# First stage of a hybrid block: later transposes for the second token block of a third, and a recurrence at 1.6 steps a block, begun at unit ten

## The chip, the cores and the metric

The kernel runs on one core of one Trainium2 chip. A core has a matmul engine (TensorE, PE in the rows of a profile, with its weight loads as PEld), a vector engine (DVE), a scalar engine (ACT), GpSimd (POOL) and SyncE (SP), whose queue issues nearly all DMAs here. Each engine works through its own list of instructions in a fixed order and stops where the next one has to wait. The metric is the device time of one execution, in microseconds (us); less is better.

## The reference, cut to what matters

One layer over T = 2064 tokens (16 learned meta tokens and 2048 of the input) of width 1024, all in float32:

```python
h = concat([meta, x])                         # (2064, 1024)
p = rms_norm(h, norm_mix_pre) @ w_in          # columns of three head groups
oa = rg_lru_group(...)        # gated linear recurrence over time, 256 columns
ob = forgetting_attention_group(q, k, v, f)   # 8 heads of 64, causal
oc = rwkv7_group(...)         # state S <- S*w - (S kk)(kk a) + v k, one step a token, 256 columns
mixed = concat([oa, ob, oc]) @ w_out
h = h + rms_norm(mixed, norm_mix_post)
f = causal_dwconv(rms_norm(h, norm_ffn_pre) @ ffn_up, ffn_conv)
h = h + rms_norm((gelu(gate) * val) @ ffn_down, norm_ffn_post)
```

The change is in how the first product, `rms_norm(h) @ w_in`, and the two recurrences that read it (`oc`, here called the recurrence, with `oa` beside it) are laid out in time. What is computed stays the same.

## The kernel before, in words

A float32 product is made of three matmuls in a shorter format: every operand is kept as a high and a low half (`xh`, `xl`, `wh`, `wl`), and L174, L175 and L176 multiply high by high, low by high and high by low. The first stage (the projection) computes `p` transposed, with 128 columns of `w_in` as the stationary operand and up to 400 tokens moving.

The tokens are cut into three thirds ("parts" in the code, 0 to 2), and each third into two token blocks: 400 and 384 tokens, 384 and 384, 256 and 256. For a third, `w_in_norm` loads token tiles of 128 rows (L127), takes the sum of squares on ACT (L119) and a short chain on DVE (L86 to L95), scales the tile (L132), and `transpose_split` turns it on PE (L145, eight transposes of 128x128 for a tile, four to a PSUM bank, tile `pst`), after which ACT writes the high half (L151) and DVE the low half (L152). The operands `xh0`, `xl0` (first block) and `xh1`, `xl1` (second block) have one buffer each, and the raw token tiles share four buffers (pool `nt`).

Then `w_in_part` runs 25 units over the third: first the eight forget-gate columns (`w_in_gate`, matmuls L293 and L294 into `psf`), then 24 units of 128 columns (8 of kind "c" for the recurrence, 4 "a" for the gated linear one, 4 each of k, v and q). A unit is one step (24 matmuls into `psp`) for each token block, and results go to DRAM. The weights of a unit are split once, in the first third, and read back ready-made in the others. From the first to the last third the two steps of a unit have 400 + 384, 384 + 384 and 256 + 256 tokens.

The recurrence reads these results back. It works on nine blocks of 256 tokens (the ninth has 64), three to a third. Written as a generator (`recurrences`), it is cut into steps: two for the forget gates of the third, then for each block four steps of preparation (its matmuls are L1040, L1051, L1115, L1144; then fifteen rounds between POOL and DVE, L1162 and L1163), ten steps that end the block before (L1186, L1228, L1238, L1253, L1265, L1273, L1304, L1309, L1333), and four of the linear recurrence (L1424, L1425). `Beside` is the pace-maker: after each projection step `advance()` adds `PACE` to a count and runs that many whole steps of the generator. The generator of a third is put in when 14 units of it are done, in the first third as in the others. What is left over after the last third is run by `beside.finish()`, ahead of the attention in the program.

The program's text is not the final order. A scheduler places every instruction, engine by engine: what stands earlier in the text has precedence, and what is not ready by its reckoning lets later work past. So recurrence matmuls stand between projection matmuls, and after the projection between those of the attention. The attention (L561 maxima, L688 and L689 scores, L711 values) takes heads in two halves of query blocks; when its first half is done, matmuls of the output projection (`pswo`) fill PE beside its second half.

Of the kernel before, what the change touches and what calls it, by code (L numbers as in the profile page):

```python
# [119 lines left out]
    return rstd_from(core.nc, v, ss, width, core.apart)  # L120


def norm_transpose(core, pools, psum, src, rows, gain, pieces, after=nullcontext):

    nc = core.nc
    xt = pools["nt"].tile([P, D], F32, tag="nt_x", name=core.n("xt"))
    nc.sync.dma_start(xt[:rows], src)  # L127
# [4 lines left out]
    nc.vector.scalar_tensor_tensor(xt[:rows], xt[:rows], rs, gain[:rows], op0=ALU.mult, op1=ALU.mult)  # L132
    transpose_split(core, psum, xt, rows, pieces)


def transpose_split(core, psum, xt, rows, pieces):

    nc = core.nc
    for k0 in range(0, KD, 4):
        ps = psum.tile([P, 4, P], F32, tag="mm", name=core.n("pst"))
        for k in range(4):
            nc.tensor.transpose(  # L145
                ps[:, k, :rows], xt[:rows, (k0 + k) * P : (k0 + k + 1) * P], core.ident[:rows, :rows]
            )
        ks = slice(k0, k0 + 4)
        for hi, lo, c, r0, n in pieces:
            ds_, ss_ = slice(c, c + n), slice(r0, r0 + n)  # L150
            nc.scalar.activation(hi[:, ks, ds_], ps[:, :, ss_], AF.Copy)  # L151
            nc.vector.tensor_tensor(lo[:, ks, ds_], ps[:, :, ss_], hi[:, ks, ds_], op=ALU.subtract)  # L152
# [36 lines left out]
def w_in_norm(core, pools, psum, x, meta, gain, part):  # L189
    blocks = []  # L190
    for b, tl in enumerate(w_in_tokens(part)):
        t0 = tl[0][0]
        n = sum(r for _, r in tl)
        hi = pools["xn"].tile([P, KD, n], F32R, tag=f"xh{b}", name=core.n("xh"))
        lo = pools["xn"].tile([P, KD, n], F32R, tag=f"xl{b}", name=core.n("xl"))
        blocks.append((t0, n, tl, hi, lo))
    for t0, n, tl, hi, lo in blocks:
        for s, rows in tl:
            src = meta if s < META else x[s - META : s - META + rows, :]
            late = part == 1 and (s, rows) not in blocks[0][2][:2]  # L200
            after = (lambda: core.tc.issue_after(core.rounded.ins)) if late else nullcontext
            norm_transpose(core, pools, psum, src, rows, gain, [(hi, lo, s - t0, 0, rows)], after)
    return blocks


def w_in_kept(scr, c0):
# [65 lines left out]
    return turn  # L272


def w_in_gate(core, pools, psum, w_in, blocks, scr, part):

    nc = core.nc
    c0 = 2048
    w = pools["w"].tile([P, KD, P], F32R, tag="wh", name=core.n("fw"))
    flat, kept = w[:].rearrange("p k c -> p (k c)").bitcast(F32), w_in_kept(scr, 3 * D)[0]  # L280
    if part == 0:
        raw = pools["st"].tile([P, KD, 8], F32, tag="stv", name=core.n("fraw"))
        nc.sync.dma_start(raw[:], w_in[:, c0 : c0 + 8].rearrange("(k p) c -> p k c", p=P))
        nc.vector.memset(w[:].bitcast(F32), 0.0)
        nc.scalar.activation(w[:, :, 0:8], raw[:], AF.Copy)
        nc.vector.tensor_tensor(w[:, :, 32:40], raw[:], w[:, :, 0:8], op=ALU.subtract)
        nc.sync.dma_start(kept, flat)
    else:
        nc.sync.dma_start(flat, kept)
    for t0, n, tl, hi, lo in blocks:  # L290
# [9 lines left out]
    yield False  # L300
    yield True


def w_in_part(core, pools, psum, w_in, blocks, scr, part):
    yield from w_in_gate(core, pools, psum, w_in, blocks, scr, part)
    units = [("c", 2056 + P * i) for i in range(8)] + [("a", P * i) for i in range(4)]
    units += [(s, c + P * i) for s, c in (("k", 1024), ("v", 1536), ("q", 512)) for i in range(4)]
    waiting = [None]

    def step(*args):  # L310

        after = w_in_step(core, pools, psum, *args, scr)
        if waiting[0]:
            waiting[0]()
        waiting[0] = after

    for kind, c0 in units[:-2]:
        w = w_in_weights(core, pools, w_in, c0, scr, part)
        for block in blocks:
            step(w, block, kind, c0)  # L320
            yield block is blocks[-1]

    last = [(w_in_weights(core, pools, w_in, c0, scr, part), kind, c0) for kind, c0 in units[-2:]]
    for block in blocks:
        for w, kind, c0 in last:
            step(w, block, kind, c0)
            yield kind == "q" and c0 == last[-1][2]
# [1681 lines left out]


READY = 13
PACE = 1.25

WIDE = (0, 5)

# [5 lines left out]
class Beside:  # L2021
# [54 lines left out]
def hybrid_block_kernel(ctx: ExitStack, tc: tile.TileContext, args, out):  # L2076
# [25 lines left out]
    with ExitStack() as p1:  # L2102
# [7 lines left out]
        with ExitStack() as p1a:  # L2110
# [4 lines left out]
            split_out = w_out_split(core, pools["nt"], a["w_out"], scr)  # L2115
            following = w_in_norm(core, pools, ps_mm, x, meta, g_pre, 0)
            for part in range(3):
                blocks = following
# [5 lines left out]
                units = w_in_part(core, pools, ps_mm, a["w_in"], blocks, scr, part)  # L2124
                for _ in range(READY if part == 0 else 0):
                    while not next(units):
                        pass
# [19 lines left out]
                    beside = Beside(PACE)  # L2147
                i = READY + 1 if part == 0 else 1
                for whole in units:
                    if whole and i == READY + 1:  # L2150
                        beside.add(recurrences(core, R, lk, a["fox_f_bias"], scr, blocks, part))
                    beside.advance()
                    if not whole:
                        continue
                    if part == 1 and i > 1:
                        next(split_out, None)
                    if part and i % 2 == 0:
                        with tc.issue_after(core.loaded.ins):
                            next(sums, None)
                    i += 1  # L2160
# [184 lines left out]
```

## Time and profile before

| what | us |
|---|---|
| median of 3 runs | 3020.2 (3015.82 to 3026.11) |
| the profiled execution | 3012.84 |
| its span, first to last instruction | 3011.1 |
| last projection matmul of the first, second, last third ends | 278.5, 613.1, 874 |
| first projection matmul of the second third starts | 321.1 |
| last recurrence matmul ends | 1125 |
| first output projection matmul starts | 1193 |

The times of the last four rows are read from the timeline of PE in the trace. A row of the table by stretches gives the stretch, its length, then for each engine its busy time and the number of its records, the mean granted PE clock (1.00 is full speed), the DMA share and the rate. With a tile's or a line's name it counts the instructions on that tile or line alone. The records of recurrence matmuls are those on the tiles `rps` and `eps`; many of them are float32 and leave two records for one matmul.

### The profile page before, as it was taken

To read this page: it belongs to the slowest core of one execution; us is meant where nothing else is said; L and a number is where in the kernel's file an instruction comes from. 1 tells how busy PE (TensorE), PEld (TensorE's weight loads), DVE (VectorE), ACT (ScalarE), POOL (GpSimd) and SP (SyncE) were. 2 spreads that over 40 slices of the span, in tenths; PEclk is the share of its full clock that TensorE was granted. 3 is DMA by queue.
4 is the path that set the end of the run, shared out by engine and by line. 5 is a ranking of instruction groups with operands and counts; after the bars stand their busy time and mean duration, and the time that the engine had idled before them with its cause. 6 is when DMAs were issued, how large, how long until landed. Compare 5 with 4: busy or idle time off the path is not lost.

```text
span 3011.1 us, 52783 instructions
## 1 busy us (share of the span) xinstructions
PE 2901.2 (96%) x18694; PEld 2487.0 (83%) x18694; DVE 2039.1 (68%) x3937; ACT 1479.4 (49%) x2858; POOL 1314.8 (44%) x1567
## 2 busy tenths in 40 slices
PE   6999999999999999999989999999999999999998
PEld 6998899888886654566558999999999999787887
DVE  5258645665577775555626898798778777656766
ACT  4246333444346654454635666666666665424333
POOL 1002121222124666566843567455644534656443
PEclk8999999999978999999999999999999999999999
DMA  6776569576653347435326565577777764436453
GB/s 212 236 240 217 164 227 310 183 236 218 188 135 81 97 109 212 111 96 124 82 76 230 167 203 177 171 209 211 215 210 218 214 199 131 162 116 220 139 180 119
DMA packets 469190, 530.49 MB, mean 176 GB/s; under 512 B 85710, under 2 KB 355736, under 8 KB 467372
## 3 DMA queue, kind: packets, MB, share of 16 engines
q1 hardware_dynamic: 468156, 526.17, 57.9%
q8 instruction: 147, 2.41, 0.3%
q14 instruction: 119, 0.97, 0.1%
q0 software_dynamic: 768, 0.93, 0.1%
HBM read 368.07 MB, written 158.90 MB: 175 GB/s over the span
## 4 chain that ended last, share of the span: by engine, by line
PE 44%; DVE 2%; DMA 1%; POOL 1%; ACT 1%; issue 1%; SPq 0%; DVEq 0%; POOLq 0%; ACTq 0%
PE psu L174 9%; PE psu L175 9%; PE psu L176 9%; PE psd L174 4%; PE psd L175 4%; PE psd L176 4%; PE pswo L174 1%; PE pswo L176 1%; PE pswo L175 1%; PE pst L1604 1%; DMA uq<-scr_us 0%; POOL dw L1638 0%; DVE uw L1638 0%; PE po L711 0%; POOL u L1903 0%
## 5 line engine op out<-in xcount | busy, mean ns | idle before, releaser
L174 PE MATMUL psu<-xo,uw 128*128 128x344 f32 x1848 | 586.6, 322 | 6.4 <-ACT ga L1809 3.3
L175 PE MATMUL psu<-xo,uw 128*128 128x344 f32 x1848 | 592.2, 321 | 0.0
L176 PE MATMUL psu<-xo,uw 128*128 128x344 f32 x1848 | 581.8, 320 | 0.0
L174 PE MATMUL psp<-xh,wh 128*128 128x384 f32 (+2 forms) x1152 | 380.4, 330 | 0.0
L176 PE MATMUL psp<-xh,wl 128*128 128x384 f32 (+2 forms) x1152 | 377.9, 328 | 0.2 <-DMA wl<-scr_wk 0.2
L175 PE MATMUL psp<-xl,wh 128*128 128x384 f32 (+2 forms) x1152 | 377.2, 327 | 0.0
L1638 DVE TENSOR_TENSOR uw<-uq,uw 128x512 fp32r<-128x512 f32 x341 | 324.9, 957 | 58.0 <-ACT uw L1637 55.2
L174 PEld LDWEIGHTS psu<-xo,uw 128*128 128x128 f32 x1848 | 346.4, 188 | 8.1 <-ACT ga L1809 3.6
L175 PEld LDWEIGHTS psu<-xo,uw 128*128 128x128 f32 x1848 | 347.7, 188 | 0.0
L176 PEld LDWEIGHTS psu<-xo,uw 128*128 128x128 f32 x1848 | 346.2, 188 | 0.0
L1637 ACT ACTIVATE uw<-uq 128x512 fp32r<-128x512 f32 x462 | 288.1, 627 | 94.0 <-PE psu L176 42.9
L693 ACT ACTIVATE p<-sc,bias 128x512 f32<-128x512 f32 (+4 forms) x352 | 197.4, 589 | 187.4 <-PE sc L689 161.4
L566 DVE TENSOR_REDUCE mc<-mx 128x1 f32<-128x512 f32 (+6 forms) x352 | 190.2, 565 | 112.8 <-PE mx L561 85.8
L1777 DVE SCALAR_TENSOR_TENSOR uy<-psu,ffn_cols,uy 128x342 f32<-128x342 f32 (+1 forms) x390 | 220.4, 567 | 59.9 <-ACT uy L1775 57.9
L1785 POOL TENSOR_TENSOR uy<-uy,uy 128x342 f32<-128x342 f32 (+1 forms) x132 | 145.4, 1102 | 240.6 <-DVE uy L1777 59.7
L732 POOL TENSOR_TENSOR acc<-acc,p 128x512 f32<-128x512 f32 (+3 forms) x208 | 221.3, 1067 | 52.1 <-DVE acc L732 24.7
L1638 POOL TENSOR_TENSOR uw<-uq,uw 128x512 fp32r<-128x512 f32 x121 | 177.9, 1470 | 138.8 <-ACT uw L1637 121.1
L174 PEld LDWEIGHTS psp<-xh,wh 128*128 128x128 f32 x1152 | 220.0, 191 | 8.3 <-issue 6.9
L176 PEld LDWEIGHTS psp<-xh,wl 128*128 128x128 f32 x1152 | 219.8, 191 | 7.6 <-issue 5.1
L175 PEld LDWEIGHTS psp<-xl,wh 128*128 128x128 f32 x1152 | 219.9, 191 | 5.0 <-issue 3.2
L1638 DVE TENSOR_TENSOR fo<-u,fo 128x896 fp32r<-128x896 f32 x88 | 101.7, 1155 | 132.0 <-ACT fo L1637 131.5
L1637 ACT ACTIVATE fo<-u 128x896 fp32r<-128x896 f32 x88 | 81.2, 923 | 205.9 <-PE psd L176 117.3
(483 smaller groups left out, 6415.2 us busy)
## 6 DMA issues: line engine op xcount, KB each, us to landing
uq<-scr_us SPq DMA_DIRECT2D x220, 256.0 KB
uq<-in_ffn_up_dram SPq DMA_DIRECT2D x209, 256.0 KB
wl<-scr_wk SPq DMA_DIRECT2D x48, 512.0 KB
wh<-scr_wk SPq DMA_DIRECT2D x48, 512.0 KB
u<-scr_ff SPq DMA_DIRECT2D x88, 256.0 KB
scr_ff<-uy SPq DMA_DIRECT2D x110, 171.0 KB
raw<-in_w_in_dram SPq DMA_DIRECT2D x24, 512.0 KB
scr_wk<-wh SPq DMA_DIRECT2D x24, 512.0 KB
```

What stands on the lines that cost most here:

```text
L174: nc.tensor.matmul(out, ah, bh, start=first, stop=False, skip_group_check=more)
L175: nc.tensor.matmul(out, ah, bl, start=False, stop=False, skip_group_check=more)
L176: nc.tensor.matmul(out, al, bh, start=False, stop=last, skip_group_check=more)
L566: self.reduced = nc.vector.tensor_reduce(mc[:rows, i, ci : ci + 1], ps[:rows, : e - a], axis=AX.X, op=ALU.max)
L693: last = nc.scalar.activation(p[:rows, :w], ps[:rows, :w], AF.Exp, bias=bias[:rows, j : j + 1])
L732: eng.tensor_tensor(a, ps_[0][0][:rows, c0:n] if start and i == 1 else a, p[:rows, : n - c0], op=ALU.add)
L1604: nc.tensor.transpose(ps[:, k, :rows], xt[:rows, k0 : k0 + P], core.ident[:rows, :rows])
L1637: core.nc.scalar.activation(hi, src, AF.Copy)
L1638: (eng or core.nc.vector).tensor_tensor(lo, src, hi, op=ALU.subtract)
L1777: core.conved = stt(y[:, :n], src[:, i : n + i], cw[:, 44 * i + cc : 44 * i + cc + 1], y[:, :n], op0=ALU.mult, op1=ALU.add)
L1785: core.pooled = nc.gpsimd.tensor_tensor(v[:, :n], g[:, :n], v[:, :n], op=ALU.mult)
```

## The change

There are four parts.

- `norm_transpose` is split into `normed` (load, norm, scale) and the transposes. In the second and third third the token tiles of the second token block are normed where they were, but their transposes are put off until the first block has gone through the gate and the first unit.
- The gate is no longer a pass over both blocks ahead of the units. Its matmuls for a block stand ahead of that block's step of the first unit. The yields of the first unit are such that the count of units stays the same.
- `PACE` goes from 1.25 to 1.6 steps of the recurrence for each projection step.
- In the second and third third the generator is put in after ten units in place of fourteen. In the first third it stays at fourteen.

```diff
-def norm_transpose(core, pools, psum, src, rows, gain, pieces, after=nullcontext):
+def normed(core, pools, src, rows, gain, after=nullcontext):
...
-    transpose_split(core, psum, xt, rows, pieces)
+    return xt
...
-    for t0, n, tl, hi, lo in blocks:
+    waiting = []
+    for b, (t0, n, tl, hi, lo) in enumerate(blocks):
...
-            norm_transpose(core, pools, psum, src, rows, gain, [(hi, lo, s - t0, 0, rows)], after)
-    return blocks
+            xt = normed(core, pools, src, rows, gain, after)
+            waiting.append((core, psum, xt, rows, [(hi, lo, s - t0, 0, rows)]))
+            if part == 0 or b == 0:
+                transpose_split(*waiting.pop())
+    return blocks, waiting
...
     for kind, c0 in units[:-2]:
         w = w_in_weights(core, pools, w_in, c0, scr, part)
         for block in blocks:
+            if gate:
+                gate(block)
+                yield block is blocks[-1]
             step(w, block, kind, c0)
+            while normed:
+                transpose_split(*normed.pop(0))
             yield block is blocks[-1]
+        gate = None
...
-PACE = 1.25
+PACE = 1.6
...
-                    if whole and i == READY + 1:
+                    if whole and i == (10 if part else READY + 1):
                         beside.add(recurrences(core, R, lk, a["fox_f_bias"], scr, blocks, part))
```

Where PE goes over from the first to the second third, the end of its list before reads as follows (`pst` are transposes of token tiles, `rps` and `eps` recurrence matmuls, `psf` the gate, `psp` the projection; numbers are buffers).

```order
L1040 MATMUL eps_3340<-rwwa_3315,wa_up 128x256 x2
L145 MATMUL pst_3226<-ident,xt_3211 128x128 x4
L145 MATMUL pst_3233<-ident,xt_3211 128x128 x4
L1051 MATMUL eps_3348<-rwsq_3345,gat 4x256 x2
L1186 MATMUL rps_2573<-rwxf_2341,rwxu_2297 32x32 x16
L1228 MATMUL rps_2591<-rww_202_1645,rwsc_1644 64x64 x8
L145 MATMUL pst_3255<-ident,xt_3240 128x128 x4
L145 MATMUL pst_3262<-ident,xt_3240 128x128 x4
L293 MATMUL psf_3271<-xh_3091,fw_3269 128x384
L294 MATMUL psf_3271<-xl_3092,fw_3269 128x384
```

The first gate matmul stands behind the transposes of all six tiles; no `psp` matmul of the second third stands ahead of these rows. After the change (line numbers are 6 higher for the gate and 12 higher from L330 on) the gate of the first block comes behind the third tile:

```order
L1156 MATMUL rps_2128<-ident,rwbk_2030 128x128 x4
L1156 MATMUL rps_2134<-ident,rwrav_2023 128x128 x4
L145 MATMUL pst_3476<-ident,xt_3454 128x128 x4
L299 MATMUL psf_3534<-xh_3392,fw_3528 128x384
L1198 MATMUL rps_2227<-rwxu_2218,rwsc_1644 32x32 x32
L1052 MATMUL eps_2970<-rwwa_2951,wa_up 128x256 x2
L300 MATMUL psf_3534<-xl_3393,fw_3528 128x384
```

and the other three tiles come behind the 24 matmuls of the first unit's first step:

```order
L174 MATMUL psp_3594<-xh_3392,wh_3530 128x384
L175 MATMUL psp_3594<-xl_3393,wh_3530 128x384
L176 MATMUL psp_3594<-xh_3392,wl_3531 128x384
L145 MATMUL pst_3622<-ident,xt_3483 128x128 x4
L145 MATMUL pst_3629<-ident,xt_3483 128x128 x4
L145 MATMUL pst_3636<-ident,xt_3498 128x128 x4
L145 MATMUL pst_3643<-ident,xt_3498 128x128 x4
L1198 MATMUL rps_2411<-rwxf_2225,rwxu_2218 32x32 x16
L1240 MATMUL rps_2466<-rww_202_1645,rwsc_1644 64x64 x8
L145 MATMUL pst_3650<-ident,xt_3513 128x128 x4
```

So 24 of the 48 transposes moved behind 16 gate and 24 projection matmuls. The second to third crossing moves in the same way, with 16 of 32 transposes.

The other place is the end of the projection on PE. Before, behind the last `psp` matmul stands the end of the sixth recurrence block, with its late lines L1253 to L1304:

```order
L175 MATMUL psp_10080<-xl_6567,wh_9817 128x256
L176 MATMUL psp_10080<-xh_6566,wl_9818 128x256
L1238 MATMUL rps_9191<-rww_973_7341,rwxf_8880 64x128 x4
L1253 MATMUL rps_9237<-rwsc_7340,rwxu_9169 64x128 x8
L1091 MATMUL eps_9753<-rwsq_9660,bones 128x512
L1253 MATMUL rps_9248<-rwsc_7340,rwxu_9169 64x128 x8
L1265 MATMUL rps_9260<-rww_973_7341,rwsc_7340 64x64 x16
L1273 MATMUL rps_9260<-rstate,rwgt_9235 64x64 x4
L1304 MATMUL rps_9298<-rstate,rwrav_7292 64x64
```

After the change it is the seventh block that begins its ending there (L1198 was L1186), and the preparation of the ninth (L1052, 64 tokens) stands beside it:

```order
L175 MATMUL psp_10681<-xl_7194,wh_10439 128x256
L176 MATMUL psp_10681<-xh_7193,wl_10440 128x256
L1156 MATMUL rps_9391<-ident,rwbk_9311 128x128 x4
L1156 MATMUL rps_9397<-ident,rwrav_9304 128x128 x4
L1156 MATMUL rps_9403<-ident,rwbk_9311 128x128 x4
L1156 MATMUL rps_9409<-ident,rwrav_9304 128x128 x4
L1198 MATMUL rps_9491<-rwxu_9482,rwsc_8363 32x32 x32
L1052 MATMUL eps_10196<-rwwa_10177,wa_up 128x64 x2
L1198 MATMUL rps_9558<-rwxu_9482 32x32 x16
L1198 MATMUL rps_9576<-rwxu_9482 32x32 x32
```

Counted over the whole built list of PE, 2304 recurrence matmuls are there in both kernels. Before, 668 of them stand behind the last projection matmul, after the change 557. The fourth block, the first of the second third, begins behind 1867 of the 3456 projection matmuls before, behind 1637 after. The last recurrence matmul stands behind 108 of the attention's 352 score matmuls of L688 before, behind 63 after; the first output projection matmul stands behind 146 and behind 152 of them.

More of the change, by code (lines that the diff above doesn't have):

```diff
@@ L272, in w_in_step, with w_in_gate @@
     return turn
-def w_in_gate(core, pools, psum, w_in, blocks, scr, part):
+def w_in_gate(core, pools, psum, w_in, scr, part):
     nc = core.nc
@@ L289, in w_in_gate, with step @@
         nc.sync.dma_start(flat, kept)
-    for t0, n, tl, hi, lo in blocks:
+    def step(block):
+        t0, n, tl, hi, lo = block
         ps = psum.tile([P, 512], F32, tag="mm", name=core.n("psf"))
@@ L299, in w_in_gate, with w_in_part @@
         nc.sync.dma_start(scr["f"][:, t0 : t0 + n], o[:, :n])
[L300 to L305, printed above, removed]
+    return step
+def w_in_part(core, pools, psum, w_in, blocks, scr, part, normed):
+    gate = w_in_gate(core, pools, psum, w_in, scr, part)
     units = [("c", 2056 + P * i) for i in range(8)] + [("a", P * i) for i in range(4)]
@@ L2117, in hybrid_block_kernel @@
             for part in range(3):
-                blocks = following
+                blocks, late = following
                 if part == 0:
@@ L2123, in hybrid_block_kernel @@
                         nc.gpsimd.dma_start(scr["p"][r : r + P, 0:PAD], zeros[:])
-                units = w_in_part(core, pools, ps_mm, a["w_in"], blocks, scr, part)
+                units = w_in_part(core, pools, ps_mm, a["w_in"], blocks, scr, part, late)
                 for _ in range(READY if part == 0 else 0):
```

## The prediction

> **What bounds the kernel now.** I read the page first, then stretches of the first stage, then who waits for whom.
>
> ```profile
> span 3011.1 us, 52783 instructions
> PE 2901.2 (96%) x18694; PEld 2487.0 (83%) x18694; DVE 2039.1 (68%) x3937; ACT 1479.4 (49%) x2858; POOL 1314.8 (44%) x1567
> PE   6999999999999999999989999999999999999998
> PEclk8999999999978999999999999999999999999999
> ```
>
> PE is busy for 96% of the span, so its work is the bound nearly everywhere. A change that only moves work can win back two things: time in which PE is idle, and time in which it runs at less than its full clock. The clock row shows the second in the 12th and 13th of its 40 slices of 75 us, where the projection hands over to the attention. Finer stretches show more (length; PE, PEld, DVE, ACT, POOL busy; clock; DMA):
>
> ```profile
> 278.50:321.10 42.60, 37.01 (x388) 30.56 (x387) 37.22 (x101) 26.67 (x51) 13.59 (x20) 0.72 0.39 119
> 288.60:312.50 23.90, 21.73 (x257) 17.19 (x250) 20.96 (x63) 16.25 (x31) 9.40 (x13) 0.50 0.26 91
> 613.10:619.70 6.60, 4.42 (x35) 3.58 (x34) 5.33 (x12) 4.99 (x12) 2.96 (x4) 1.00 0.90 268
> 619.70:623.10 3.40, 3.40 (x18) 3.40 (x17) 2.21 (x6) 0.47 (x2) 0.00 (x0) 0.50 1.03 395
> 628.30:874.00 245.70, 239.83 (x2572) 218.58 (x2571) 158.07 (x405) 107.58 (x220) 57.68 (x91) 0.98 0.61 188
> 874.00:1047.00 173.00, 162.24 (x1489) 113.89 (x1488) 132.10 (x368) 93.45 (x208) 85.90 (x137) 0.81 0.44 104
> 1047.00:1125.00 78.00, 72.40 (x528) 45.11 (x527) 59.93 (x155) 46.56 (x96) 47.03 (x74) 0.98 0.43 101
> 1125.00:1193.00 68.00, 60.36 (x272) 30.32 (x271) 39.98 (x88) 29.71 (x54) 36.45 (x43) 0.90 0.78 218
> ```
>
> The first row is the crossing from the first to the second third, from the last projection matmul of the one to the first of the other. In its 42.6 us PE is idle for 5.6 us, and at a clock of 0.72 it loses about 0.28 x 42.6 = 12 us more (one of them counted already, since 2.2 us of the half-clock stretch in the second row are idle). The crossing loses 16.5 us. The other crossing loses 2.2 us idle (third row) and half of 3.4 us at half clock (fourth): 3.9 us. The last third (fifth row) loses little. Behind the projection, 874 to 1193, what is left of the recurrence runs among the attention's first half, and the clock is 0.81 to begin with.
>
> How the attention and the recurrence share that time is seen by counting: score matmuls of L688 (PE, PEld only), then recurrence matmuls on `rps`, then on `eps`, in two stretches each:
>
> ```profile
> 874.00:1047.00 173.00, 24.40 (x62) 12.18 (x63) 0.81 0.44 104
> 1047.00:1125.00 78.00, 18.65 (x52) 9.05 (x51) 0.98 0.43 101
> 1125.00:1193.00 68.00, 13.91 (x34) 6.32 (x33) 0.90 0.78 218
> 1450.00:1500.00 50.00, 15.90 (x41) 7.48 (x41) 1.00 0.33 73
> ...
> 874.00:1047.00 173.00, 67.44 (x1046) 56.82 (x1044) 25.71 (x57) 12.19 (x25) 0.81 0.44 104
> 1047.00:1125.00 78.00, 13.90 (x220) 10.33 (x220) 7.34 (x24) 2.91 (x7) 0.98 0.43 101
> ...
> 874.00:1047.00 173.00, 8.88 (x36) 5.55 (x36) 3.13 (x9) 4.08 (x12) 0.81 0.44 104
> ```
>
> Until 1125 us PE executes 1046 + 220 + 36 = 1302 recurrence records and 114 score matmuls. Then 34 scores take 68 us without any recurrence, and late in the attention 41 scores take 50 us, with nothing beside them.
>
> **The change part by part.** First the price of a recurrence record inside the projection, from the last third (tiles `rps`, then `eps`):
>
> ```profile
> 628.30:874.00 245.70, 74.54 (x1346) 62.43 (x1347) 33.92 (x68) 19.26 (x38) 0.98 0.61 188
> 628.30:874.00 245.70, 23.63 (x85) 12.46 (x85) 9.62 (x23) 10.89 (x26) 0.98 0.61 188
> ```
>
> That is 98.2 us for 1431 records, 69 ns each. Behind the projection it is (67.44 + 8.88 + 13.90) / 1302, again 69 ns. The built lists put 668 recurrence matmuls behind the last projection matmul before, 557 after; 668 are 1302 records, so the 111 moved are 216 records.
>
> *Pace and earlier start, cost.* The projection ends later by 216 x 69 ns = 14.9 us: PE is full there, so nothing hides them. The last third's idle time, 245.7 - 239.8 = 5.9 us on 1431 records, adds 4 ns to each, 1 us. Sum +16. DVE and ACT carry their share beside it (158 and 108 us busy of 246). A step brings its DMAs to SP with it, but PE's waits for weights in these thirds come to one row (below).
>
> *Pace and earlier start, gain.* After the change the attention reaches its 63rd score with 557 x 1.95 = 1086 records done; before, it reached the 62nd at 1047 us with 1082 done. The same work in the same mixture: 173 us, no gain. From there to the 114th it took 78 us beside 220 records; now none are left. Two rows bound what that saves. If PE sets the pace, the records' own 13.9 us go. If the attention then runs as at 1450 us, 52 scores take 52 x 50 / 41 = 63.4 us, and 14.6 us go. If the chain of maxima, exponentials and sums sets the pace, nothing goes. I take -14, because PE was busy for 72.4 of the 78 us, and keep 0 and -15. From the 114th score on nothing changes: the first output projection matmul stands behind 146 scores before and 152 after.
>
> *Late transposes, first crossing.* Nothing is removed: 48 transposes, 32 gate matmuls and the recurrence stay. But the first gate matmul no longer stands behind the sixth tile, whose transposes ran at 308.8:
>
> ```profile
> 280.90 1.07 ACT L151 ACTIVATE xh<-pst 128x512 fp32r<-128x512 f32 x2
> 281.98 1.28 DVE L152 TENSOR_TENSOR xl<-pst,xh 128x512 fp32r<-128x512 f32 x2
> 284.22 1.15 SPq L127 DMA_DIRECT2D xt<-in_x_dram  x2
> ...
> 300.31 1.97 PE L145 MATMUL pst<-ident,xt 128*128 128x128 f32 x8 [0.47 <-DVE xt L132]
> 308.77 1.97 PE L145 MATMUL pst<-ident,xt 128*128 128x128 f32 x8
> 321.13 0.34 PE L174 MATMUL psp<-xh,wh 128*128 128x384 f32 x1
> ```
>
> The last two tiles were late because their loads wait for raw buffers that the first two tiles free, and went out at 284.2 (third row here). Meanwhile 40 dense matmuls (16 gate, 24 projection) now fill PE, so the half clock should end some 10 us sooner than at 312.5. I take 5 us of lost clock and 3 us of idle time as what remains of the 16.5 (the first three tiles' copies, 1.3 us a tile on DVE by the row at 281.98, still stand between their transposes and the gate): -8.5. Bounds: -3, if copying keeps PE waiting, and -14.
>
> *Second crossing.*
>
> ```profile
> 612.98 3.62 PE L145 MATMUL pst<-ident,xt 128*128 128x128 f32 x28
> 618.76 0.66 PE L145 MATMUL pst<-ident,xt 128*128 128x128 f32 x4 [2.16 <-DVE xl L152]
> ```
>
> There 28 transposes ran at once and PE then waited 2.16 us for a bank. Now 16 go, with four banks, and recurrence matmuls stand in the hole. Of 3.9 us I take -3; bounds 0 and -4.
>
> *Gate inside the first unit, first third.* The same matmuls in another order; no transpose moves. 0, hidden by nothing and needing nothing; at worst a weight that is late, 0.2 us by the row below.
>
> Sum: +16 - 14 - 8.5 - 3 = -9.5. The profiled execution took 3012.8 (span 3011.1 and 1.7 around it), 7.4 under the median, so the like execution would take 3003.3, and the median goes to 3020.2 - 9.5, about 3010. The extremes of the terms give +16 - 0 - 3 - 0 = +13 and +16 - 15 - 14 - 4 = -17.
>
> A rule speaks against this. The Trainium skill, "TensorE: Matmul & The Clock Gate", section "Part 4: PE-mode transpose", says that transposes do not count as busy time for the clock. The fourth row above agrees: after 32 transposes the clock is halved for 3.4 us, although it stayed full while they ran.
>
> **The rivals.**
>
> *Transposes in the middle cost a clock window.* The late transposes stand between dense matmuls, 24 of them with 36 small recurrence matmuls about them at the first crossing. If such a stretch halves the clock once, as at 619.7, each crossing pays half of 3.4 us: 2 x 1.7 = 3.4, hence -6, 3014. The rule quoted is this mechanism. For it: the fourth row. Against it: the transposes of the first crossing are now split in two.
>
> *The attention's chain is the limit.* Then the last 52 scores gain nothing: +16 - 11.5 = +4.5, 3025. For it: 1125 to 1193, 34 scores in 68 us, half a score a us, slower than with the recurrence. Against it: 41 in 50 us later, and that slow stretch is where the attention changes halves and DMA is at 0.78.
>
> *The recurrence stalls the projection, and it gets slower.* In the lists after the change the blocks follow each other by 340 to 370 projection matmuls in the second third (377 to 442 before), as close as their own dependencies let them in the scheduler's reckoning. A recurrence matmul that is not ready holds up the projection behind it. The waits of PE from 150 to 874 us were small:
>
> ```profile
> PE rps L1186 <- DVE rwxu L1203: 6.5, 5, 2.1
> PE rps L1186 <- ACT rwsc L1145: 1.9, 2, 1.7
> PE psp L176 <- DMA wl<-scr_wk: 0.2, 1, 0.2
> ```
>
> But where the recurrence runs unpaced, 874 to 1047, PE is idle for 10.8 of 173 us, 6.2%, against 2.4% in the last third. If the projection from 281 to 874 us goes the same way, it loses 3.8% of 593 = 22 us: +13, 3033. It decides once PE's idle share there is up by 1.6% (9.5 us). The Trainium skill, in the same page under "Part 2: What happens when you issue a matmul", says that matmuls stay in program order; the waits above are that order at work.
>
> *The handover warms up.* The 0.81 of 874 to 1047 is 33 us of lost clock. If dense projection matmuls up to the end and a shorter tail save a third of it, the gain is 20: 3000 or less.
>
> **How the numbers follow.** Chances: the forecast 0.50 (its own range 2998 to 3022: -17 and, with both crossings at their lesser bounds, -1, and some 4 us of scatter at each end), transposes that cost a window 0.08, the attention's chain 0.14, stalls 0.22, a warmer handover 0.06. About 0.3%, 9 us, is what a measurement of this kernel can tell from no change; the runs shown spread by 10. Of the forecast 0.38 lies under 3011, since its largest unknowns (how long the clock stays halved at the first crossing, what a moved record costs) reach further down. With the warm handover that makes faster 0.44. Within 9 us: the rest of the forecast 0.12, transposes 0.08, most of the attention's chain 0.10, 0.30. Slower: stalls 0.22 and 0.04 of the chain, 0.26. The range runs from 2995, which takes in the forecast and a part of the warm handover, to the stalls' 3033, and leaves out half of the stalls.
>
> **What would show it.** Right: at the first crossing a half clock that ends before 303 us in place of 312.5; the projection ending near 878 (874 + 16 - 11.5); recurrence matmuls ending near 1050; the first output projection matmul near 1183. Wrong: a PE idle share over 4% from 330 us to the projection's end, or waits of `psp` or `rps` there of 15 us or more in all; the first output projection matmul behind 1193 in spite of a projection that ends on time.

## The result and the profile after

The kernel got slower. Over 16 runs of each, the median is 3028.9 us after the change (3023.96 to 3046.66) and 3018.1 us before (3012.41 to 3026.11): ratio 1.0044, 95% interval 1.0034 to 1.0055. The profiled execution took 3028.55 us. The page of the kernel after, to set beside the one shown of before:

```profile
span 3026.7 us, 52801 instructions
PE 2904.5 (96%) x18694; PEld 2497.7 (83%) x18694; DVE 2034.5 (67%) x3937; ACT 1483.2 (49%) x2858; POOL 1315.2 (43%) x1567
PE   6999999999998988999989999999999999999998
PEclk8999999999996989999999999999999999999999
```

Every engine has the work that it had. The dip of the clock where the projection hands over to the attention stands in the 13th of 40 slices, with a smaller one in the 15th, in place of the 12th and 13th, since the projection ends later. The page doesn't show where 16 us went; stretches cut at the same places of the program do. They are, first before and then after: 50 us from the end of the first third's projection, the inside of the second third, 20 us around the second crossing, the inside of the last third, and from the projection's end to the first output projection matmul (columns as in the prediction: length; busy us of PE, PEld, DVE, ACT, POOL; clock; DMA).

```profile
278.50:328.50 50.00, 44.41 (x445) 36.89 (x445) 42.55 (x113) 28.29 (x55) 14.11 (x21) 0.76 0.37 112
328.50:608.10 279.60, 277.35 (x2316) 253.99 (x2313) 151.82 (x368) 97.58 (x183) 56.13 (x83) 0.99 0.72 237
608.10:628.10 20.00, 17.82 (x145) 16.56 (x144) 13.73 (x36) 7.60 (x17) 2.96 (x4) 0.91 0.92 311
628.10:873.70 245.60, 239.73 (x2572) 218.48 (x2572) 158.07 (x405) 107.49 (x220) 57.68 (x91) 0.98 0.61 189
873.70:1193.00 319.30, 295.30 (x2287) 189.61 (x2287) 232.01 (x610) 169.96 (x356) 169.38 (x252) 0.87 0.51 128
```

```profile
277.10:327.10 50.00, 46.85 (x535) 39.72 (x534) 43.85 (x114) 28.06 (x56) 14.57 (x22) 0.97 0.50 161
327.10:634.60 307.50, 296.14 (x2478) 268.63 (x2478) 181.20 (x453) 122.99 (x232) 64.71 (x98) 0.96 0.68 220
634.60:654.60 20.00, 19.87 (x206) 17.22 (x199) 16.11 (x33) 7.09 (x14) 4.03 (x5) 0.83 0.55 183
654.60:910.80 256.20, 246.58 (x2485) 223.89 (x2485) 149.19 (x385) 94.79 (x197) 49.28 (x77) 0.96 0.59 180
910.80:1217.30 306.50, 275.89 (x2091) 179.62 (x2090) 209.17 (x551) 163.78 (x338) 169.91 (x253) 0.88 0.51 133
```

Length less PE's busy time is idle time, and length times what the clock lacks to 1.00 is lost clock; their sum is called the loss below (the clock taken unrounded from the trace). Two things about it: idle time inside a stretch of half clock is counted in both terms (up to 1.7 us in a row shown here), and half clock comes in stretches of 3.4 us or multiples of it in the projection here, so the lost clock goes in steps of 1.7 us. In the first row the loss falls from 17.5 to 4.9 us: the first crossing gained. In the second row it rises from 4.0 to 25.0: 11.4 us idle where 2.3 were, and 13.7 us of lost clock where 1.7 were. In the fourth it rises from 11.7 to 19.9. The projection ended at 910.8 us in place of 873.7. The last row got 13 us shorter, and what follows it 9 us (4 and 11 in a second profile of each kernel).

What PE waited for in the two thirds after the change, and how the longest wait comes about: first the five largest of PE's waits from 327 to 911 us (us in total, times, longest), then ACT's and PE's instructions around one of them, then the stretch behind it.

```profile
PE eps L1052 <- ACT rwe L1054: 5.6, 2, 3.0
PE rps L1198 <- DVE rwix L1175: 4.9, 2, 2.9
PE rps L1198 <- DVE rwxu L1215: 2.8, 1, 2.8
PE psp L174 <- DMA wh<-scr_wk: 2.6, 1, 2.6
PE eps L1436 <- ACT rwlg L1440: 1.7, 1, 1.7
```

```profile
513.11 0.47 ACT L244 ACTIVATE sth<-psp 128x384 fp32r<-128x384 f32 x1
513.59 1.28 ACT L1452 ACT_TABLE_LOAD   x1
514.89 0.42 ACT L1452 ACTIVATE rwlr<-rwlr 128x256 f32<-128x256 f32 x1
515.32 1.28 ACT L1054 ACT_TABLE_LOAD   x1
516.62 0.84 ACT L1054 ACTIVATE rwe<-eps,rwkv_om 128x256 f32<-128x256 f32 x2
...
514.16 0.34 PE L175 MATMUL psp<-xl,wh 128*128 128x384 f32 x1
517.51 1.22 PE L1052 MATMUL eps<-rwwa,wa_up 64*128 64x256 f32 x2 [3.01 <-ACT rwe L1054]
```

```profile
515.60:522.50 6.90, 4.99 (x13) 4.16 (x14) 5.95 (x12) 4.32 (x9) 4.70 (x7) 0.51 0.37 109
```

The second pair of matmuls of L1052 needs the one `eps` buffer, which L1054 on ACT has to empty first. On ACT stands, in between, an instruction of the gated linear recurrence (L1452) that uses another function table. So the table is exchanged twice, 1.28 us each time, PE stands still for 3.0 us with projection matmuls queued behind, and its clock is halved for 6.9 us, from 1.1 us into the wait on. The kernel before loads tables about as often in these thirds (31 times, 32 after) and has no wait of PE for ACT above 0.2 us from 328 to 874 us; so it isn't their number, but where they stand. (The Trainium skill, "ScalarE: Activation LUTs", section "What ACT_TABLE_LOAD costs", gives 1283 ns for the load and about 1380 ns more for a drain. The load agrees, but here ACT was busy until 513.58 and again from 514.89, so that no such drain shows.)

The waits for DVE are of the same kind. PE's row and DVE's list ahead of it, for one of them:

```profile
832.78 1.22 DVE L1071 TENSOR_TENSOR rwe<-rwe 128x512 f32<-128x512 f32 x1
834.30 0.25 DVE L1175 TENSOR_REDUCE rwix<-rwitmp 128x8 f32<-128x88 f32 x1 [0.30 <-POOL rwitmp L1174]
834.47 0.52 DVE L1097 COPY rwwc<-rwe 128x8 f32<-128x8 f32 x1
834.90 0.41 DVE L1462 SCALAR_TENSOR_TENSOR rwlr<-rwlr,rwlraw 128x256 f32<-128x256 f32 x1
835.35 0.54 DVE L1463 SCALAR_TENSOR_TENSOR rwlu<-rwlu,rwlr 128x256 f32<-128x256 f32 x1
835.82 0.67 DVE L1215 TENSOR_TENSOR rwxu<-rps,rwxu 32x512 f32<-32x512 f32 x1
...
836.55 0.68 PE L1198 MATMUL rps<-rwxu,rwsc 32*32 32x32 f32 x9 [2.83 <-DVE rwxu L1215]
```

L1215 is a step in the end of one block. Ahead of it stands work of other blocks: preparation (L1071, L1097), a round (L1175, which waited for POOL in its turn) and the linear recurrence (L1462, L1463).

### The profile page after: what moved, and what is told of

Its sections match the earlier page's. It is cut to its first block, busy times and chain, and to the rows that moved or that the text cites. A ratio compares the mean times of both kernels' runs of the same rounds, so it can differ in the third digit from the quotient of the medians.

```text
span 3026.7 us, 52801 instructions
## 1 busy us (share of the span) xinstructions
PE 2904.5 (96%) x18694; PEld 2497.7 (83%) x18694; DVE 2034.5 (67%) x3937; ACT 1483.2 (49%) x2858; POOL 1315.2 (43%) x1567
## 5 line engine op out<-in xcount | busy, mean ns | idle before, releaser
L1174 POOL TENSOR_TENSOR rwitmp<-rwix,rwia 128x16 f32<-128x16 f32 (+9 forms) x135 | 67.6, 501 | 268.9 <-DVE rwia L1169 189.7
```

What stands on the lines that cost most here:

```text
L1174: nc.gpsimd.tensor_tensor(m3, x3[:, :, : t + 1], a3[:, t : t + 1, : t + 1].to_broadcast([np_, jw, t + 1]), op=ALU.mult)
```

## The experiments

All experiments share one set of measures: the ratio to the kernel before, and the loss by the four stretches named above. At the outset there were three theories. T1: the recurrence at its new pace and start stalls the projection, and the gain at the crossings is real. T2: the new order of the transposes costs by itself. T3: nothing stalls; work was moved and the gains were given back elsewhere.

The results together (us of loss; two values are two profiles of the same kernel; "order" names the thirds that have the late transposes):

| kernel | pace, start, order | first crossing | inside second third | second crossing | inside last third | ratio to before |
|---|---|---|---|---|---|---|
| before | 1.25, 14, none | 17.5, 18.5 | 4.0, 5.7 | 3.9, 1.5 | 11.7, 10.3 | 1 |
| after | 1.6, 10, both | 4.9, 7.0 | 25.0, 26.7 | 3.5, 0.0 | 19.9, 17.8 | 1.0044 [1.0034, 1.0055] |
| e_order | 1.25, 14, both | 8.7 | 4.0 | 4.0 | 20.2 | 0.9987 [0.9968, 1.0005] |
| e_rec | 1.6, 10, none | 19.0 | 12.0 | 6.5 | 15.0 | 1.0047 [1.0030, 1.0063] |
| e_pace | 1.6, 14, both | 5.3 | 15.0 | 3.2 | 18.5 | 1.0010 [0.9989, 1.0030] |
| e_start | 1.25, 10, both | 9.3 | 3.9 | 7.9 | 22.1 | 1.0013 [0.9995, 1.0030] |
| e_alone | none in the last two thirds, both | 7.0 | 1.1 | 0.4 | 12.9 | 1.0492 [1.0478, 1.0506] |
| e_lru | 1.6, 10, both | 7.0 | 13.4 | 8.4 | 10.5 | 1.0230 [1.0215, 1.0246] |
| e_half | 1.25, 14, second | 12.3 | 2.9 | 2.0 | 14.8 | 0.9974 [0.9956, 0.9991] |
| e_slow | 1.0, 14, both | 9.4 | 4.4 | 4.8 | 8.2 | 1.0067 [1.0054, 1.0081] |
| e_mid | 1.4, 14, second | 8.7 | 12.6 | 2.1 | 14.4 | 1.0004 [0.9989, 1.0019] |
| e_last | 1.6, 10, second | 4.5 | 30.2 | 0.0 | 13.1 | 1.0038 [1.0026, 1.0051] |

**The parts apart.** Four kernels, each with a part of the change. The order alone:

```diff
-PACE = 1.6
+PACE = 1.25
...
-                    if whole and i == (10 if part else READY + 1):
+                    if whole and i == READY + 1:
```

> The order of the second token block alone (pace 1.25, generator put in after 14 units, as in the kernel before). Theory 1, the recurrence stalls the projection: the crossings keep what the changed kernel's trace shows there (a loss of 5.9 us between 250 and 350 us in place of 17.3), the rest of the projection is as before, so 8 to 12 us less than before, a ratio of 0.996 to 0.997. Theory 2, the order itself costs (raw buffers and projection banks held longer, the second crossing split into small pieces): the projection ends 10 us or more later than 874 us and the ratio is 1.003 or more. Theory 3, only moved work is paid for and the crossing's gain is given back in the tail: 0.999 to 1.001.

The recurrence alone, from the kernel before:

```diff
-PACE = 1.25
+PACE = 1.6
...
-                    if whole and i == READY + 1:
+                    if whole and i == (10 if part else READY + 1):
```

> The recurrence alone (pace 1.6, generator put in after ten units in the last two thirds; gate and transposes as in the kernel before). Theory 1: the stalls without the crossings' gain, so slower than the changed kernel: a ratio of 1.006 to 1.009 to the kernel before, the projection ends near 920 us, and PE's idle and half-clock time in the projection outside the crossings is 20 us or more above before. Theory 2: this part is harmless, 0.998 to 1.001. Theory 3: 15 us more projection, 13 less tail, 1.000 to 1.001.

The kernel after with the start back at fourteen units (e_pace), and with the pace back at 1.25 (e_start):

> The changed kernel with the generator put in after 14 units again (pace 1.6 and the order stay). The built list puts 655 recurrence matmuls behind the projection, as the order alone does, so the pace moves little work. Theory 1 with the pace as the cause of stalls: 1.003 or more. Theory 1 with the early start as the cause: 0.996 to 0.998, like the order alone.

> The changed kernel with a pace of 1.25 (the start after ten units and the order stay). The built list puts 557 recurrence matmuls behind the projection, as the changed kernel's does. Theory 1 with the pace as the cause of stalls: the stalls go, the moved work and the tail's gain stay, 0.995 to 0.998. Theory 1 with the early start as the cause: 1.003 to 1.005, like the changed kernel.

The recurrence alone gives the whole slowdown, 1.0047 beside 1.0044, so T1 holds in the main, though its own forecast for this kernel, 1.006 to 1.009, was missed. The order alone isn't slower, which speaks against T2, but its gain, 0.13%, isn't told from nothing, and is less than T1 forecast. Pace and start each cost about a quarter of a per cent beside the order alone, though the intervals overlap, and neither came out in one of the ranges given for it. Inside the second third they differ (order alone, then pace 1.6, then start at ten):

```profile
326.60:599.50 272.90, 270.58 (x2271) 247.52 (x2270) 150.39 (x367) 97.09 (x182) 55.64 (x82) 0.99 0.73 238
```

```profile
326.00:605.90 279.90, 273.42 (x2223) 250.13 (x2222) 149.75 (x365) 97.67 (x182) 58.54 (x82) 0.97 0.71 229
```

```profile
326.20:615.90 289.70, 287.47 (x2445) 262.33 (x2444) 171.36 (x432) 112.74 (x212) 57.35 (x93) 0.99 0.72 231
```

With the higher pace the third holds no more recurrence (1551 records from crossing to crossing in both), yet idle time goes from 2.3 to 6.5 us and lost clock from 1.7 to 8.5. With the early start 225 records more stand in the third, PE does 174 instructions more in this stretch, and the loss stays at 3.9. So here the start moves work, as priced, and the pace makes stalls: PE's waits in this stretch are one of 2.1 us with the order alone, and with pace 1.6 among others 2.6 us of L1052 for ACT and 1.6 and 1.0 of L1198 for DVE. Both together make more than their sum: 25 us. Over the whole of the two thirds the picture is less clean: the loss is 36.9 us with the order alone, 41.9 with the pace and 43.3 with the start, whose loss comes at the second crossing and in the last third. Which of the two costs more isn't settled.

e_rec shows one thing that none of the theories had said (its first crossing, then the inside of its second third):

```profile
281.30:331.30 50.00, 42.91 (x445) 35.58 (x444) 41.35 (x110) 28.39 (x55) 11.80 (x22) 0.76 0.33 105
331.30:636.60 305.30, 298.43 (x2568) 271.56 (x2568) 181.10 (x449) 122.03 (x230) 64.82 (x95) 0.98 0.69 225
```

Its first crossing lost 19.0 us, as before, and the inside of its second third 12.0; after the change it was 4.9 and 25.0. The sums are 31.0 and 29.9. With this pace and start, what the order gained at the crossing was lost again inside the third, while at the old pace (e_order) it was kept. That the recurrence's instructions on DVE and ACT catch up while PE stands still at a crossing would explain it; it is argued, not shown.

**How much recurrence, and what it waits for.** Four more. Without steps of the recurrence in the last two thirds:

```diff
-                    beside.advance()
+                    if part == 0:
+                        beside.advance()
```

> The kernel after the change, but no step of the recurrence is handed out beside the projection of the last two thirds; the scheduler still lets 443 of the recurrence's matmuls in there, where 1665 stand after the change and 1554 before. Between the projection ends of the first and of the last third, PE's idle time and lost clock together were 36.6 us before and 53.0 after. Queue theory (recurrence matmuls wait for DVE and ACT, stop the projection and cool the clock): that sum falls to 20 or less, and the two thirds take 425 us or less in place of 634. Rival (the projection's own loads and the two crossings make the loss): the sum stays above 30, and the thirds take 440 or more. The whole kernel gets slower in both, 3030 to 3100, since more recurrence stands behind the projection.

The loss of the two thirds is 21.4 us, a little above the 20 of the queue theory and well below its rival's 30; 7.7 of it are one wait of PE for ACT's copy of a result of the projection (`psv`), and the inside of the second third loses 1.1 us. The thirds took 434.8 us, between the two forecasts. The kernel took 3165 us, more than I allowed for. From this kernel to the one after, 2349 records came into the two thirds (851 and 3200), and their time without the loss went from 413.4 to 580.4 us: 71 ns a record.

With the linear recurrence of the last six blocks put off:

```diff
-        yield from lru_block(core, R, scr, lk, b)
+        if part:
+            core.put_off.append(lru_block(core, R, scr, lk, b))
+            for _ in range(4):
+                yield
+        else:
+            yield from lru_block(core, R, scr, lk, b)
...
         beside.finish()
+        for gen in core.put_off:
+            run(gen)
```

> The kernel after the change, but the gated linear recurrence of the last six blocks is put off until behind the projection, with empty steps in its place, so that the pace of the other recurrence stays the same. Its work is nearly all on DVE and ACT. Queue theory (recurrence matmuls are late because the instructions they wait for stand behind other blocks' work in the queues of DVE and ACT): idle time and lost clock of the last two thirds fall from 53 to 42 or less, and these thirds get 10 us shorter or more. Rival (the recurrence's own chain of dependencies is late, whatever else stands in the queues): the sum stays at 48 to 58, and the thirds get shorter only by the records of the linear recurrence. The whole time isn't disputed: 3015 to 3045.

The loss fell from 53.3 to 39.3 us and the thirds from 633.7 to 605.0, which is the queue theory's side. ACT loads 15 tables in these thirds in place of 32. PE's four largest waits from 326 to 605 us are, with the linear recurrence gone:

```profile
PE rps L1198 <- DVE rwxu L1215: 2.0, 1, 2.0
PE rps L1198 <- DVE rwix L1175: 1.3, 1, 1.3
PE psp L176 <- DMA wl<-scr_wk: 1.2, 1, 1.2
PE psp L174 <- DMA wh<-scr_wk: 1.1, 1, 1.1
```

The wait for L1054 is gone, the waits for DVE are not. In the longest of them other work still stands ahead on DVE, a split of weights of the output projection (L1497) and a round that waited for POOL (L1175):

```profile
400.79 1.56 DVE L1497 TENSOR_TENSOR wo<-raw,wo 128x1024 fp32r<-128x1024 f32 x1
402.72 0.27 DVE L1175 TENSOR_REDUCE rwix<-rwitmp 128x8 f32<-128x112 f32 x1 [0.37 <-POOL rwitmp L1174]
402.90 0.67 DVE L1215 TENSOR_TENSOR rwxu<-rps,rwxu 32x512 f32<-32x512 f32 x1
...
403.63 0.56 PE L1198 MATMUL rps<-rwxu,rwsc 32*32 32x32 f32 x12 [1.96 <-DVE rwxu L1215]
```

So about half of the loss inside the second third (26 to 13) hangs on the linear recurrence, and the rest on what is left in the queues, as here, or on the recurrence's own chain; over the whole stretch these two weren't told apart. The whole kernel took 3087 us, which I had not foreseen: six linear recurrences in a row behind it made the stretch from the projection's end to the first output projection matmul 87 us longer.

The order in the second third alone (e_half, whose edit is shown), and the order in both thirds with a gentler pace (e_slow: pace 1.0, start at fourteen):

```diff
-            if part == 0 or b == 0:
+            if part != 1 or b == 0:
...
-PACE = 1.6
+PACE = 1.25
...
-                    if whole and i == (10 if part else READY + 1):
+                    if whole and i == READY + 1:
```

> The new order at the first crossing alone: pace 1.25, start at fourteen units, and the last third transposed as before. If the order of the last third itself is what gave the gain of the first crossing back (273.6 us for that third, 260.5 before), the last third takes 258 to 264 and the ratio to before is 0.995 to 0.998. If the last third's loss comes from stalls that fall differently in each build, it takes 265 to 275 again, and the ratio is 0.998 to 1.001.

> The new order with a gentler recurrence, pace 1.0 and start at fourteen units; 788 recurrence matmuls stand behind the projection, 655 with the order alone. Queue theory: fewer steps beside the projection, fewer stalls; the two thirds take 260 moved records x 71 ns = 18 us less and another 3 to 8 us less for stalls, and the tail gives back 14 to 18: ratio to before 0.995 to 0.999. Rival (a longer tail costs what it saves or more): 1.000 to 1.004.

e_half is the only kernel whose interval lies below 1: 3007.6 us, ratio 0.9974 [0.9956, 0.9991]. That is the ratio of the first expectation with the last third of the second (267.0 us), so it didn't separate the two readings. Nor does its profile show where the gain lies: the profiled execution took 3013.9 us, and its two thirds 597.5 us, where the two profiles of the kernel before have 595.2 and 594.4. The gain rests on the runs alone. e_slow came out above both of its ranges, and goes against the queue theory's sum: the two thirds did get shorter by 24 us against e_order, but what stands behind the projection got 44 us longer, where 14 to 18 were expected. The rows from the projection's end to the first output projection matmul, of e_slow and then e_order:

```profile
852.20:1219.10 366.90, 326.01 (x2545) 214.66 (x2544) 259.58 (x679) 194.96 (x401) 173.59 (x261) 0.83 0.45 114
```

```profile
878.10:1194.30 316.20, 288.11 (x2263) 186.09 (x2263) 230.13 (x605) 169.50 (x355) 167.96 (x251) 0.88 0.50 128
```

267 records more behind the projection (1541 and 1274) cost 44 us from its end to the kernel's, 164 ns each; 219 fewer, after the change, saved 18 us, 83 ns each. A record behind the projection hasn't one price. The clock there, 0.83 and 0.88, is one part of it.

**What is left of pace, order and scatter.** The kernel e_half with pace 1.4, and the kernel after with the last third's transposes as before (`part != 1` again in place of `part == 0`); then the two kernels unchanged, for a second profile each.

> The order in the second third alone, start at fourteen, pace 1.4 in place of 1.25. The lists hold almost the same number of recurrence matmuls behind the projection (663 against 655), so only the spacing of the recurrence's steps differs. Theory of spacing (steps handed out closer together find their operands unfinished): between pace 1.25 and 1.6, ratio 0.997 to 1.000, and idle time with lost clock of the last two thirds 31 to 38 us. Rival (pace only matters by the records that it moves): as with 1.25, ratio 0.996 to 0.998 and 31 us or less.

> The kernel after the change with the last third transposed as before; pace 1.6 and start at ten stay. If the order of the last third costs something, this is faster than the kernel after the change by 3 to 6 us: ratio to before 1.002 to 1.0035. If it doesn't, 1.0035 to 1.0055.

> The kernel before, unchanged, for a second profile. If a third's loss is a property of the kernel, the last third takes 258 to 263 us again and idle time with lost clock of the last two thirds is 33 to 40 us. If it scatters from one execution to the next, the last third may take 265 or more.

> The kernel after the change, unchanged, for a second profile. Stalls as a property of the kernel: idle time with lost clock of the last two thirds is 46 to 60 us again, and the two thirds take 628 to 640. Scatter: below 42, with thirds of 620 or less.

The inside of the second third, of e_half and then e_mid:

```profile
327.70:603.20 275.50, 272.62 (x2301) 248.38 (x2298) 154.33 (x374) 97.12 (x182) 55.94 (x83) 1.00 0.74 240
326.90:607.00 280.10, 274.34 (x2271) 250.11 (x2270) 151.44 (x370) 98.34 (x182) 56.17 (x82) 0.98 0.71 232
```

At pace 1.4 it loses 12.6 us, at 1.25 it loses 2.9 to 5.7, with the same recurrence in it. So spacing counts, not only the work moved (with the first crossing taken in, where the higher pace loses less, it is 21.3 us for e_mid and 15.2 for e_half); the ratio, 1.0004, came out a little above the range given for that. The second profiles repeat the first: before 36.0 us of loss (37.1) and 257.5 us for the last third (260.5), after 51.5 (53.3) and 631.8 us for the two thirds (633.7). Even the places are the same: the kernel after stalled on L1052 at 517.5 and 626.0 in the first profile and at 516.3 and 625.7 in the second, and on L1198 at 836.5 and 833.7. The stalls belong to the built lists, not to an execution.

e_last doesn't decide by its ratio (the interval covers most of both expectations), but the column for the last third does, read over all kernels with the whole recurrence and a pace of 1.25 or more: with late transposes there it loses 17.8 to 22.1 us (four kernels), without them 10.3 to 15.0 (five). So the order costs some 6 us inside the last third, while the second crossing shows no gain (0.0 to 7.9 us with it, 0.0 to 6.5 without). By which wait it costs them wasn't found.

## Why the prediction was wrong, step by step

It said 3010 us and faster; it was 3029 and slower. The time lies within the range, and the sign is that of the rival "the recurrence stalls the projection". Means over the two profiles of each kernel, before and after, beside the terms:

| step of the prediction | forecast | measured |
|---|---|---|
| moved records in the projection | +15 | +15.5 (218 x 71 ns) |
| idle time with them | +1 | +21.0 inside the second third, +7.9 inside the last (idle 13.9, lost clock 15.0) |
| first crossing | -8.5 | -12.0 |
| second crossing | -3 | -1.0 |
| behind the projection | -14 | -18.1 |
| first third | 0 | -2.1 |
| in no column | | +6.5 |
| sum | -9.5 | +17.7 |

The sum is that of the profiled spans (3011.0 and 3028.8 on average); the medians differ by 10.8, since the two profiled executions of the kernel before took 5 us less than its median, and one of the kernel after 4 us more. The kernel after from the 63rd to the 114th score matmul, to set beside the row from 1047 to 1125 us in the prediction:

```profile
1074.10:1152.40 78.30, 68.03 (x328) 39.97 (x328) 47.83 (x114) 43.86 (x91) 49.62 (x80) 0.91 0.50 115
```

- *Moved records.* The number is right, 218 for 216. The price of 71 ns is the one from e_alone to the kernel after. From before to after, the time of the two thirds without the loss rose by 22.1 us, 101 ns a record; the difference is the 6.5 us in no column. Some of it may belong to the new order: e_order, with only 26 records more than before, has 6.4 us more of that time. This wasn't followed up.
- *"The last third's idle time ... adds 4 ns to each, 1 us."* This is the step that failed. It took the stalls of a spacing that the scheduler had laid out at pace 1.25 as a price per record, and scaled it by the number of records moved. In its place the runs showed 28.9 us more loss inside the two thirds, with PE waiting for ACT before L1052 and for DVE before L1198. The stalls don't go by the number of records. e_pace moved none against e_order and lost 11 us more inside the second third; e_start moved 98 matmuls more and lost nothing more there. The sign "the projection ending near 878" was missed by this: it ended at 910.8 and 906.6.
- *First crossing.* Right and a little low. The half clock ended at 290.4 us, and at 295.3 in the second profile (before 303 was the sign given), and the loss fell by 12.0, inside the bounds of 3 and 14. But with this pace and start the gain didn't last, as e_rec shows.
- *Second crossing.* 1 us in place of 3, and over all kernels no gain. The order's cost inside the last third wasn't thought of.
- *Tail.* The number is near, 18 us less where 14 were forecast, but that is luck: nothing of it came where it was forecast. From the 63rd to the 114th score matmul, which was to gain 14 us, it took 78.1 and 77.4 us before and 78.3 and 77.9 after. With the recurrence gone from it (the row above), PE's idle time rose from 5.6 to 10.3 us there and its lost clock from 1.7 to 6.8. The 18 us came elsewhere, where the forecast had nothing: 5.1 ahead of the 63rd score (10.0 in one pair of profiles, 0.3 in the other), 3.7 from the 114th to the first output projection matmul, 9.7 behind that. What made them wasn't found. The recurrence ended at 1081 in place of 1050, late by the projection's lateness.
- *The rival that came true* was worked out as 22 us of stalls and 3033 us, with a chance of 0.22. Its sign, PE's idle time up by 9.5 us, was met inside the thirds: it went from 8.1 to 21.0 us, and in the second profiles from 9.2 to 24.1. But it counted idle time alone: the lost clock there went from 7.5 to 23.9 us (6.8 to 20.5), about as much again. Together they are the 29 us. Two of my signs for "wrong" were just missed in the first profile: the idle share from 327 us to the projection's end was 3.6%, not 4, and the waits on `psp` and `rps` came to 13 us, not 15 (with those on `eps`, 21). In the second both were met, with 4.2% and 16 us.
- The evidence was there: the lists after the change put the blocks closer together, and the unpaced recurrence behind the projection showed 6.2% idle time at a clock of 0.81. I gave the stalls 0.22 and let the quiet rows of before speak for the changed kernel.
- *Transposes that cost a clock window.* Not shown. After the change the clock is halved for 3.4 us at the first crossing (286.9 to 290.4), but that is among matmuls of the first block's gate and of the recurrence; the late transposes run from 300.8 to 306.6 us, and the clock stays full there. At the second crossing it is halved for 6.8 us in one of the two profiles, from 645.4 us on, just as the first of the late transposes starts, and not at all in the other. The row on which the rival leaned, half clock from 619.7 us in the kernel before, isn't there in that kernel's second profile, with the same 32 transposes.
- *The attention's chain.* What it said came true: the last 52 scores gained nothing. The tail as a whole gained all the same, and whether the chain of maxima, exponentials and sums is what holds them wasn't tested.
- *A warmer handover.* It doesn't show: the clock from the projection's end to the first output projection matmul went from 0.87 to 0.88, and in the second profiles from 0.88 to 0.86.

## What to carry to other kernels

Work that fills an engine's list from the side is priced by how far apart its dependent steps stand, not only by how much of it there is: look at what stands ahead of its producers in the queues of the other engines. Count a stall of PE together with the half clock that follows it, here about as much again. And take a change of several parts apart: the part that paid (the order, in one third alone) was worth 0.26% (0.09 to 0.44), and the parts beside it took more. And check a forecast stretch by stretch: the tail's sum came out nearly as forecast, and the stretch that was to bring it gained nothing.

## What the runs showed of the hardware

Half clock followed short waits. In the kernel after, PE waited from 705.4 to 707.1 us, and the clock was halved at 706.8, after 1.4 us of idle time (the first row's 6.90 less 5.51, all of it in this wait):

```profile
699.90:706.80 6.90, 5.51 (x42) 4.80 (x40) 1.83 (x4) 4.94 (x9) 1.56 (x3) 1.00 0.54 187
706.80:710.20 3.40, 3.09 (x10) 2.74 (x11) 2.96 (x7) 2.83 (x5) 0.00 (x0) 0.50 0.00 0
```

Waits of 2.8 to 3.0 us were followed by 6.8 to 10.2 us of it. The Trainium skill, "TensorE: Matmul & The Clock Gate", section "HAM oscillation — how this bites in real kernels", puts the rule as no idle gaps above about 3.4 us; here the clock was halved after less than half of that, among small matmuls, though not each time: 2.11 us at 668.0 in the kernel before left the clock full, and 2.09 us at the same place in its second profile did not.
